# Differential and windowed attention: 128-row scores, rebuilt operand round trips, and PSUM shared as three and five banks

## The chip, the cores and the metric

The kernel runs on one core of one Trainium2 chip. The metric is device time in microseconds of one execution of the whole program, as the median of several runs. One execution was also recorded by the hardware profiler; all rows of the trace come from that one. The engines are TensorE (PE, with its weight loads as PEld), VectorE (DVE), ScalarE (ACT), GpSimd (POOL) and SyncE (SP), which here does no arithmetic and issues nearly all transfers.

## What is computed

Two layers of a bidirectional encoder trunk on 512 tokens of width 1024, all in float32. Each layer is, cut to what matters:

```
h = rms_norm(x)
z = h @ w_in                      # q, k, v of differential attention; q, k, v of three window groups; two gates
a = differential_attention(z_A)   # 4 heads, each with two 64-wide score maps: softmax(s0) - lambda * softmax(s1), times v
b = dilated_window_attention(z_B) # 3 groups x 8 heads of width 64, dilations 1, 4, 16; merged by softmax denominators
m = (sigmoid(g_A) * (a @ w_a) + sigmoid(g_B) * (b @ w_b)) @ w_out
x = x + rms_norm(m)
x = x + rms_norm(swiglu(rms_norm(x)))
```

Queries and keys get rotary embedding. A score is a product over 64 channels of a query and a key row. The kernel reaches float32 accuracy by splitting a number into a high part (`float32r`, rounded) and a low part (the remainder): a product of two split matrices is taken as hi x hi + hi x lo + lo x hi, three TensorE products (`mm3`, L120).

## The kernel before

The tokens are held in a permuted order, by their class modulo 4, so that the dilated groups see neighbours together; group 0 (dilation 1) needs the natural order. `class_rows` (L226) describes the permuted rows of a DRAM tensor; rows of x come in with `rows_in` (L229), four transfers of 32 rows per tile of 128 tokens, and leave at the end through `postnorm_tile` (L252), four per tile, one of them issued by GpSimd.

Weights stream from DRAM in 1 MB loads (`load_raw`, L85), are split by ScalarE and VectorE into high and low parts (`split_part`, L94), and are consumed in the order of `specs` (L321).

In a layer the first stage runs eight **units of projection**: for each half of the heads (u = 0, 1) one unit of differential attention (`da_proj`, L490), then for each half again three window groups (`g_proj`, L571). A unit projects q, k and v (`proj_qk`, `proj_v`), 48 TensorE products of 512 columns each for q and k and 96 of 256 columns for v. TensorE's order is written by hand: `drive` (L185) runs the projection as a generator and, at each of its yields (four for q, four for k, four for v), calls `att_step` (L169), which issues one step of an attention that was queued earlier. `att_push` gives each attention a delay in such steps (`DELAY`, L23: 4 for differential attention, 3 more for its first unit; 4, 2, 2 for groups 0, 1, 2). So the scores of a unit are issued a fixed number of steps after its last projection, between the products of the next units. The other engines and the transfers are ordered by a scheduler.

**The operand round trips.** A projection leaves the two rotary halves of four heads in partitions as (head, channel); the score products need channels on the partitions and the heads apart. Rope (L406) works on VectorE and GpSimd, and the result goes through DRAM scratch. In `qk_split` (L456), used by differential attention and by group 0, each of q and k is split into hi (L463, ScalarE) and lo (L465, VectorE), both are written to the scratch `dasc` (L466, L467), and loaded back in strips of 32 partitions (L474, L478, L481) into three operands: `QX` has, per head, hi and lo of q on 64 partitions each; `KX` has hi of k twice; `KL` has lo of k on 64 partitions. That makes 4 writes and 16 loads. `qk_scores` (L484) takes a score as two products: L487 contracts 128 rows (q hi and lo with k hi), L488 contracts 64 rows (q hi with k lo). A score call holds four such products, L487 and L488 in turn: two maps of 512 columns in differential attention, two windows of 256 columns in group 0. Each kind has 8 calls per unit, 2 units per layer and 2 layers.

Group 0 also sends v through the scratch `vd` (four writes, two loads, L575 to L581) into natural order, and its output back through `scr` and `scs` (`to_class`, L674). Its order is q, k, v. Groups 1 and 2 do without the split: `gsc` gets q and k in two writes, and four loads (L591) fetch both into `QK`; their scores (L616) contract 64 rows, sixteen products in a row.

All these transfers go through `move` (L423) to SyncE's queue. The operands live in the pool `big` (L429, 7 buffers of 8 KB per partition); `KL` and v live in `m4` (8 buffers).

**PSUM** has eight banks: four for projections (`pj`, L57) and four for attention (`at`, L60). `act_stationary` (L277), the last product of each sub-layer, uses all eight as accumulators, and `ws_halves` (L206) takes four projection banks for the first two products of the next stage.

Of the kernel before, what the change touches and what calls it, by code (L numbers as in the profile page):

```python
# [17 lines left out]
P = 128  # L18
D = 1024
S = 512  # L20
SPLIT_PRI = 400
MOVE_POOL = 0
DELAY = (4, 4, 2, 2, 3)  # L23
# [11 lines left out]
def encoder_trunk_kernel(  # L35
# [8 lines left out]
    depth = w_in.shape[0]  # L44
    mv = [0]

# [10 lines left out]
    def pj(shape=(P, S)):  # L57
        return ps.tile(list(shape), F32, tag="pj", name=nm("pj"))

    def at(shape=(P, S)):  # L60
        return ps.tile(list(shape), F32, tag="at", name=nm("at"))

# [143 lines left out]
    def ws_halves(jobs, tok_halves, between={}):  # L206
        step = S // tok_halves
        outs = [[pj() for _ in range(2)] for _ in jobs]
        made = {}
        for hf in range(tok_halves):  # L210
            sl = slice(hf * step, (hf + 1) * step)
            for jn, (o2, job) in enumerate(zip(outs, jobs)):
                lhs, rhs = made[jn] = made.get(jn) or job()
                for i in range(2):
                    mm3(o2[i][:, sl], [lhs(i, k) + (rh[:, sl], rl[:, sl]) for k, (rh, rl) in enumerate(rhs)])
                if (hf, jn) in between:
                    between[hf, jn]()
        return outs
# [10 lines left out]
    def rows_in(xt, src, n, permuted):  # L229
        if permuted:  # L230
            for s in range(4):
                nc.sync.dma_start(out=xt[32 * s:32 * s + 32, :], in_=class_rows(src, n)[s])
        else:
            nc.sync.dma_start(out=xt, in_=src[n * P:(n + 1) * P, :])

# [16 lines left out]
    def postnorm_tile(n, pe, src, g, dst, src_perm, dst_perm):  # L252
# [11 lines left out]
        nc.vector.scalar_tensor_tensor(out=xt, in0=t, scalar=r, in1=xt, op0=ALU.mult, op1=ALU.add)  # L264
        if dst_perm:
            for s in range(4):
                (nc.gpsimd if s == 3 else nc.sync).dma_start(out=class_rows(dst, n)[s], in_=xt[32 * s:32 * s + 32, :])
        else:
            nc.sync.dma_start(out=dst[n * P:(n + 1) * P, :], in_=xt)
        return xt, t  # L270
# [6 lines left out]
    def act_stationary(nk, lhs, post, turn, next_jobs):  # L277
        accs = [[(pj if n < 2 else at)() for _ in range(2)] for n in range(NT)]
        nch = nk // 2
# [41 lines left out]
    def specs():  # L321
# [11 lines left out]
        for l in range(depth):  # L333
            for u in range(2):
                yield from qkv(l, 256 * u, 512 + 256 * u, 1024 + 256 * u)[(1 if l == 0 and u == 0 else 0):]
            for u in range(2):
                for gi in range(3):
                    b = GB + gi * 1536 + 256 * u
                    yield from qkv(l, b, b + 512, b + 1024)

# [47 lines left out]
    for l in range(depth):  # L388
# [34 lines left out]
        def move(dst, src):  # L423
            mv[0] += 1
            eng = nc.gpsimd if MOVE_POOL and mv[0] % MOVE_POOL == 0 else nc.sync
            eng.dma_start(out=dst.bitcast(F32) if dst.dtype == F32R else dst,
                              in_=src.bitcast(F32) if src.dtype == F32R else src)

        def big(shape=(P, 4, S), dt=F32R):  # L429
            return ap.tile(list(shape), dt, tag="big", name=nm("big"), bufs=7)  # L430

# [23 lines left out]

        def qk_split(natural, first=None):  # L456
            QX, KX = big(), big()
            KL = m4([P, 2, S], F32R)
            sc = dp.tile([P, 2, 2, 2, S], F32, tag="dasc", name=nm("dasc"), bufs=2)
            for which in range(2):  # L460
                pair = rope((yield from proj_qk(which, first)), natural)
                hi = rt(F32R)
                nc.scalar.copy(out=hi, in_=pair)  # L463
                lo = rt(F32R)
                nc.vector.tensor_tensor(out=lo, in0=pair, in1=hi.bitcast(F32), op=ALU.subtract)  # L465
                move(sc[:, which, 0], hi)  # L466
                move(sc[:, which, 1], lo)  # L467
                src = sc.rearrange("(c j) w hl ab t -> w hl ab j c t", j=32)[which]
                if which == 0:
                    for hl in range(2):  # L470
                        for ab in range(2):
                            for par in range(2):
                                o = 64 * ((hl + par) % 2) + 32 * ab
                                move(QX[o:o + 32, par::2, :], src[hl, ab, :, par::2, :])  # L474
                else:
                    for ab in range(2):
                        for o in (32 * ab, 64 + 32 * ab):
                            move(KX[o:o + 32], src[0, ab])  # L478
                        for par in range(2):
                            o = 64 * par + 32 * ab  # L480
                            move(KL[o:o + 32], src[1, ab, :, par::2, :])  # L481
            return QX, KX, KL

        def qk_scores(o, qk, c, qs, ks):  # L484
            QX, KX, KL = qk
            b = 64 * (c % 2)
            nc.tensor.matmul(o, QX[:, c, qs], KX[:, c, ks], start=True, stop=False)  # L487
            nc.tensor.matmul(o, QX[b:b + 64, c, qs], KL[b:b + 64, c // 2, ks], start=False, stop=True)  # L488

        def da_proj(first):  # L490
            qk = yield from qk_split(False, first)
            return qk, (yield from proj_v())

# [77 lines left out]
        def g_proj(gi):  # L571
            if gi == 0:
                QK = yield from qk_split(True)
                v = yield from proj_v()
                vd = dp.tile([S, 256], F32, tag="vd", name=nm("vd"), bufs=2)  # L575
                for s in range(4):
                    move(vd.rearrange("(t s r) c -> s t r c", s=4, r=4)[s], v[32 * s:32 * s + 32])
                vn = m4([P, NT, 256])
                move(vn, vd.rearrange("(n p) c -> p n c", p=P))
                vs = m4([P, 3, 256])  # L580
                move(vs, vd[64:448].rearrange("(n p) c -> p n c", p=P))  # L581
                return QK, vn, vs
            QK = big((P, 2, 2, S), F32)
            sc = dp.tile([P, 2, 2, S], F32, tag="gsc", name=nm("gsc"), bufs=2)
            for which in range(2):
                move(sc[:, which], rope((yield from proj_qk(which, None)), False))
            src = sc.rearrange("(pair par j) w ab t -> par ab j w pair t", par=2, j=32)
            for par in range(2):
                for ab in range(2):
                    o = 64 * par + 32 * ab  # L590
                    move(QK[o:o + 32], src[par, ab])  # L591
            return QK, (yield from proj_v()), None

# [80 lines left out]
        def to_class(o, st):  # L674
# [4 lines left out]
            oc, sc = g_out(0)  # L679
            for s in range(4):  # L680
                move(oc[32 * s:32 * s + 32], scr.rearrange("(t s r) c -> s t r c", s=4, r=4)[s])
                move(sc[32 * s:32 * s + 32], scs.rearrange("(t s r) c -> s t r c", s=4, r=4)[s])
            return oc, sc
# [216 lines left out]
```

## Time and profile before

| what | value |
|---|---|
| median of 3 runs (lowest, highest) | 1938.34 us (1934.69, 1938.78) |
| the profiled execution | 1938.61 us |
| its span, first to last instruction | 1936.8 us |
| granted TensorE clock, mean of the span | 0.994 |
| DMA: all 16 engines, share of the span in which the hardware queue moved data | 41.2% |
| moved | 244.92 MB |

The median, not the mean, is the number to be predicted. In the page, "busy" is the time in which an engine worked on at least one instruction. TensorE's products overlap in the records: a product is shown until its result is out, while the next has begun, so its pace is read from start to start. In the view of waits, a row names the engine and the line that waited, what ended the wait, the total, the number of waits and the longest. In the rows of DMA issues the last number is the median time from issue to landing. In the table of windows the columns are the stretch, its length, the busy time of each engine with the number of its instructions, the granted clock, the busy share of the 16 DMA engines and GB/s.

### The profile page before, as it was taken

The numbers are of one execution on the slowest core, as the hardware profiler recorded it, in microseconds if no ns is written. First come the engines' busy times: TensorE is split into PE (matmuls) and PEld (weight loads), VectorE is DVE, ScalarE is ACT, GpSimd is POOL, SyncE is SP. The second block draws the span as 40 slices with busy tenths as digits, with TensorE's granted clock in tenths as the row PEclk, the third lists the DMA queues.
The fourth block names the chain that finished last, engine by engine and source line by source line (L and its number), as shares of the span: only waits on it lengthen the run. The fifth ranks groups of instructions, "written<-read, shape, count | busy, mean of one in ns | idle before, by whom it ended". The sixth has DMA issues, their size and how long they took to land. (4 is left out here: it accounts for less than half of the span.)

```text
span 1936.8 us, 24393 instructions
## 1 busy us (share of the span) xinstructions
PE 1889.4 (98%) x9952; PEld 1586.0 (82%) x9952; DVE 929.5 (48%) x1243; ACT 671.5 (35%) x1301; POOL 179.9 (9%) x136
## 2 busy tenths in 40 slices
PE   6999999999999999999999999999999999999997
PEld 6878887888888888888887788878888888888886
DVE  4676556544545333332366765556453453333222
ACT  3354333344224322221334544323432342222221
POOL 1111013011100000000011211121100000000000
PEclk9999999999999999999999999999999999999999
DMA  6844446442244332322448254554323432323232
GB/s 176 253 127 131 121 120 185 129 121 87 87 163 153 109 109 87 103 94 88 162 151 233 88 151 120 151 162 130 100 89 137 144 131 89 107 87 109 87 119 65
DMA packets 171871, 244.92 MB, mean 126 GB/s; under 512 B 10864, under 2 KB 136176, under 8 KB 171760
## 3 DMA queue, kind: packets, MB, share of 16 engines
q1 hardware_dynamic: 171568, 242.84, 41.2%
q8 instruction: 78, 1.28, 0.3%
q0 software_dynamic: 192, 0.52, 0.1%
q14 instruction: 33, 0.27, 0.0%
HBM read 205.52 MB, written 37.81 MB: 126 GB/s over the span
## 5 line engine op out<-in xcount | busy, mean ns | idle before, releaser
L123 PE MATMUL pj<-hTh,whi 128*128 128x512 f32 (+1 forms) x1600 | 610.1, 381 | 3.0 <-ACT hTh L248 3.0
L124 PE MATMUL pj<-hTl,whi 128*128 128x512 f32 (+1 forms) x1600 | 600.2, 375 | 6.0 <-DVE hTl L249 5.9
L125 PE MATMUL pj<-hTh,wlo 128*128 128x512 f32 (+1 forms) x1600 | 599.6, 375 | 0.0
L109 DVE TENSOR_TENSOR wlo<-raw,whi 128x1024 fp32r<-128x1024 f32 x252 | 341.1, 1355 | 489.4 <-ACT whi L108 480.4
L108 ACT CAST whi<-raw 128x1024 fp32r<-128x1024 f32 x252 | 264.7, 1051 | 771.2 <-PE pj L124 498.6
L123 PEld LDWEIGHTS pj<-hTh,whi 128*128 128x128 f32 x1600 | 304.0, 190 | 62.7 <-ACT hTh L248 5.2
L124 PEld LDWEIGHTS pj<-hTl,whi 128*128 128x128 f32 x1600 | 304.3, 190 | 58.0 <-DVE hTl L249 7.7
L125 PEld LDWEIGHTS pj<-hTh,wlo 128*128 128x128 f32 x1600 | 304.1, 190 | 54.6
L123 PE MATMUL pj<-whi,hTh 128*128 128x256 f32 x512 | 148.5, 290 | 0.0
L125 PE MATMUL pj<-whi,hTl 128*128 128x256 f32 x512 | 144.8, 283 | 0.0
L124 PE MATMUL pj<-wlo,hTh 128*128 128x256 f32 x512 | 144.8, 283 | 0.0
L634 ACT ACTIVATE e<-e,gst 128x128 f32<-128x128 f32 (+1 forms) x192 | 81.9, 428 | 140.0 <-DVE gst L631 139.9
L77 POOL TENSOR_TENSOR sm<-sm,mhalf 128x1 f32<-128x1 f32 (+1 forms) x48 | 28.7, 599 | 970.1 <-DVE sm L75 970.1
L123 PEld LDWEIGHTS pj<-whi,hTh 128*128 128x128 f32 x512 | 97.9, 191 | 6.0 <-issue 3.7
L124 PEld LDWEIGHTS pj<-wlo,hTh 128*128 128x128 f32 x512 | 98.0, 191 | 0.0
L125 PEld LDWEIGHTS pj<-whi,hTl 128*128 128x128 f32 x512 | 98.0, 191 | 0.0
L825 DVE TENSOR_TENSOR s<-s,pj 128x512 f32<-128x512 f32 x44 | 30.3, 689 | 123.7 <-PE pj L125 123.6
L420 POOL TENSOR_TENSOR r<-r,r 128x512 f32<-128x512 f32 x32 | 43.0, 1344 | 453.3 <-DVE r L418 332.8
L418 DVE TENSOR_TENSOR r<-pj,cos 128x512 f32<-128x512 f32 x48 | 32.9, 690 | 77.4 <-PE pj L125 77.4
L419 POOL TENSOR_TENSOR r<-r,r 128x512 f32<-128x512 f32 x32 | 64.5, 2015 | 25.0 <-DVE r L418 25.0
L487 PE MATMUL at<-big,big 128*128 128x256 f32 (+1 forms) x128 | 55.3, 432 | 9.6 <-DMA vd<-m 7.5
L287 PE MATMUL pj<-whi,ac 128*128 128x512 f32 x160 | 63.0, 394 | 0.0
(166 smaller groups left out, 2482.0 us busy)
## 6 DMA issues: line engine op xcount, KB each, us to landing
raw<-in_w_in_dram SPq DMA_DIRECT2D x64, 1024.0 KB, 7.0
raw<-in_w_gate_up_dram SPq DMA_DIRECT2D x44, 1024.0 KB, 5.1
raw<-in_w_down_dram SPq DMA_DIRECT2D x22, 1024.0 KB, 4.8
dasc<-r SPq DMA_DIRECT2D x32, 512.0 KB, 3.5
big<-dasc SPq DMA_DIRECT2D x64, 128.0 KB, 6.6
big<-dasc SPq DMA_DIRECT2D x32, 256.0 KB, 8.0
gsc<-r SPq DMA_DIRECT2D x16, 512.0 KB, 3.5
big<-gsc SPq DMA_DIRECT2D x32, 256.0 KB, 7.3
```

The source lines that it names most:

```text
L108: nc.scalar.copy(out=shp(hi), in_=src)
L109: nc.vector.tensor_tensor(out=shp(lo), in0=src, in1=shp(hi.bitcast(F32)), op=ALU.subtract)
L123: nc.tensor.matmul(o, ah, bh, start=(i == 0), stop=False)
L124: nc.tensor.matmul(o, ah, bl, start=False, stop=False)
L125: nc.tensor.matmul(o, al, bh, start=False, stop=(i == n - 1))
L287: nc.tensor.matmul(o, al, hi[:, sl], start=False, stop=False)
L418: nc.vector.tensor_tensor(out=dst[:, i], in0=u, in1=tb, op=ALU.mult)
L419: nc.gpsimd.tensor_tensor(out=pair[:, 0], in0=pair[:, 0], in1=tmp[:, 0], op=ALU.subtract)
L420: nc.gpsimd.tensor_tensor(out=pair[:, 1], in0=pair[:, 1], in1=tmp[:, 1], op=ALU.add)
L487: nc.tensor.matmul(o, QX[:, c, qs], KX[:, c, ks], start=True, stop=False)
L634: nc.scalar.activation(out=e[:, i, :], in_=e[:, i, :], func=AF.Exp, bias=sts[:, n, h:h + 1], accum_out=sts[:, n, 4 + h:5 + h])
L825: nc.vector.tensor_tensor(out=s, in0=s, in1=ou_[i], op=ALU.mult)
```

## The change

- `qk_split` becomes `split_part_of`, called once for q and once for k. The scratch holds hi and lo as 128 rows (part, rotary half, channel) by head. hi and lo are written by two transfers each, one per rotary half, and one transfer of 128 partitions fetches an operand. For k a second operand gets the same rows with the halves exchanged (two transfers of 64 partitions). Scores are then QX x KH + QX x KL with 128 rows in both products: hi x hi + lo x lo, and hi x lo + lo x hi. The product lo x lo is new.
- Group 0 projects k, v, q in this order (in `specs` and in `g_proj`).
- In groups 1 and 2, q and k are written by two transfers each (one per rotary half) and each is fetched by one.
- Rows of x, the last store, v in `vd` and the results in `scr` and `scs` take one transfer in the place of four; the last store leaves GpSimd's queue.
- PSUM: three `pj` banks and five `at` banks. `ws_halves` and `act_stationary` take their fourth projection bank from `at`.
- `big` has 8 buffers and holds K's low halves too; the scratch for DMA descriptors is set to 4096 bytes per partition.

```diff
@@ PSUM
-        return ps.tile(list(shape), F32, tag="pj", name=nm("pj"))
+        return ps.tile(list(shape), F32, tag="pj", name=nm("pj"), bufs=3)
...
-        return ps.tile(list(shape), F32, tag="at", name=nm("at"))
+        return ps.tile(list(shape), F32, tag="at", name=nm("at"), bufs=5)
...
-        outs = [[pj() for _ in range(2)] for _ in jobs]
+        outs = [[pj(), pj()], [pj(), at()]]
...
-        accs = [[(pj if n < 2 else at)() for _ in range(2)] for n in range(NT)]
+        accs = [[pj(), pj()], [pj(), at()], [at(), at()], [at(), at()]]
@@ rows of x, the last store
-        if permuted:
-            for s in range(4):
-                nc.sync.dma_start(out=xt[32 * s:32 * s + 32, :], in_=class_rows(src, n)[s])
-        else:
-            nc.sync.dma_start(out=xt, in_=src[n * P:(n + 1) * P, :])
+        nc.sync.dma_start(out=xt, in_=class_rows(src, n) if permuted else src[n * P:(n + 1) * P, :])
...
-                (nc.gpsimd if s == 3 else nc.sync).dma_start(out=class_rows(dst, n)[s], in_=xt[32 * s:32 * s + 32, :])
...
+        nc.sync.dma_start(out=class_rows(dst, n) if dst_perm else dst[n * P:(n + 1) * P, :], in_=xt)
@@ the order of the weights
-                    yield from qkv(l, b, b + 512, b + 1024)
+                    q, k, v = qkv(l, b, b + 512, b + 1024)
+                    yield from (k, v, q) if gi == 0 else (q, k, v)
@@ operands of differential attention and group 0 (qk_split goes)
+        def split_part_of(which, dsts, natural, first=None):
+            pair = rope((yield from proj_qk(which, first)), natural)
+            sc = dp.tile([P, 4, S], F32, tag="dasc", name=nm("dasc"), bufs=3)
+            rows = sc.rearrange("(hl ab j) c t -> hl ab c j t", hl=2, ab=2)
+            hi = rt(F32R)
+            nc.scalar.copy(out=hi, in_=pair)
+            for ab in range(2):
+                move(rows[0, ab], hi[:, ab, :])
+            lo = rt(F32R)
+            nc.vector.tensor_tensor(out=lo, in0=pair, in1=hi.bitcast(F32), op=ALU.subtract)
+            for ab in range(2):
+                move(rows[1, ab], lo[:, ab, :])
+            move(dsts[0], sc)
+            if len(dsts) > 1:
+                move(dsts[1][0:64], sc[64:128])
+                move(dsts[1][64:128], sc[0:64])
...
-            b = 64 * (c % 2)
-            nc.tensor.matmul(o, QX[:, c, qs], KX[:, c, ks], start=True, stop=False)
-            nc.tensor.matmul(o, QX[b:b + 64, c, qs], KL[b:b + 64, c // 2, ks], start=False, stop=True)
+            nc.tensor.matmul(o, QX[:, c, qs], KH[:, c, ks], start=True, stop=False)
+            nc.tensor.matmul(o, QX[:, c, qs], KL[:, c, ks], start=False, stop=True)
...
         def da_proj(first):
-            qk = yield from qk_split(False, first)
-            return qk, (yield from proj_v())
+            QX, KH, KL = big(), big(), big()
+            yield from split_part_of(0, (QX,), False, first)
+            yield from split_part_of(1, (KH, KL), False, first)
+            return (QX, KH, KL), (yield from proj_v())
@@ g_proj
-                QK = yield from qk_split(True)
+                QX, KH, KL = big(), big(), big()
+                yield from split_part_of(1, (KH, KL), True)
                 v = yield from proj_v()
                 vd = dp.tile([S, 256], F32, tag="vd", name=nm("vd"), bufs=2)
-                for s in range(4):
-                    move(vd.rearrange("(t s r) c -> s t r c", s=4, r=4)[s], v[32 * s:32 * s + 32])
+                move(vd.rearrange("(t s r) c -> s t (r c)", s=4, r=4), v.rearrange("p r c -> p (r c)"))
...
+                yield from split_part_of(0, (QX,), True)
+                return (QX, KH, KL), vn, vs
...
-                move(sc[:, which], rope((yield from proj_qk(which, None)), False))
-            src = sc.rearrange("(pair par j) w ab t -> par ab j w pair t", par=2, j=32)
-            for par in range(2):
-                for ab in range(2):
-                    o = 64 * par + 32 * ab
-                    move(QK[o:o + 32], src[par, ab])
+                pair = rope((yield from proj_qk(which, None)), False)
+                sc = dp.tile([P, 2, S], F32, tag="gsc", name=nm("gsc"), bufs=3)
+                for ab in range(2):
+                    move(sc.rearrange("(pj ab) pair t -> ab pair pj t", ab=2)[ab], pair[:, ab, :])
+                move(QK[:, which], sc)
@@ to_class
-            for s in range(4):
-                move(oc[32 * s:32 * s + 32], scr.rearrange("(t s r) c -> s t r c", s=4, r=4)[s])
-                move(sc[32 * s:32 * s + 32], scs.rearrange("(t s r) c -> s t r c", s=4, r=4)[s])
+            for dst, src in ((oc, scr), (sc, scs)):
+                move(dst.rearrange("p r c -> p (r c)"), src.rearrange("(t s r) c -> s t (r c)", s=4, r=4))
@@ kernel
-    nc = _bacc.Bacc("TRN2", target_bir_lowering=False, num_devices=1)
+    nc = _bacc.Bacc("TRN2", target_bir_lowering=False, num_devices=1, dynamic_dma_scratch_size=4096)
```

More of the change, by code (lines that the diff above doesn't have):

```diff
@@ L21 @@
 SPLIT_PRI = 400
-MOVE_POOL = 0
 DELAY = (4, 4, 2, 2, 3)
@@ L44, in encoder_trunk_kernel @@
     depth = w_in.shape[0]
-    mv = [0]
     pp = ctx.enter_context(tc.tile_pool(name="pp", bufs=1))
@@ L264, in postnorm_tile @@
         nc.vector.scalar_tensor_tensor(out=xt, in0=t, scalar=r, in1=xt, op0=ALU.mult, op1=ALU.add)
-        if dst_perm:
-            for s in range(4):
-                (nc.gpsimd if s == 3 else nc.sync).dma_start(out=class_rows(dst, n)[s], in_=xt[32 * s:32 * s + 32, :])
-        else:
-            nc.sync.dma_start(out=dst[n * P:(n + 1) * P, :], in_=xt)
+        nc.sync.dma_start(out=class_rows(dst, n) if dst_perm else dst[n * P:(n + 1) * P, :], in_=xt)
         return xt, t
@@ L423, in move @@
         def move(dst, src):
-            mv[0] += 1
-            eng = nc.gpsimd if MOVE_POOL and mv[0] % MOVE_POOL == 0 else nc.sync
-            eng.dma_start(out=dst.bitcast(F32) if dst.dtype == F32R else dst,
+            nc.sync.dma_start(out=dst.bitcast(F32) if dst.dtype == F32R else dst,
                               in_=src.bitcast(F32) if src.dtype == F32R else src)
         def big(shape=(P, 4, S), dt=F32R):
-            return ap.tile(list(shape), dt, tag="big", name=nm("big"), bufs=7)
+            return ap.tile(list(shape), dt, tag="big", name=nm("big"), bufs=8)
         oaT = [big() for i in range(2)]
@@ L454, in proj_v @@
             return v
[L456 to L470, printed above, removed]
-                        for ab in range(2):
-                            for par in range(2):
[L473 to L479, printed above, removed]
-                            o = 64 * par + 32 * ab
-                            move(KL[o:o + 32], src[1, ab, :, par::2, :])
-            return QX, KX, KL
@@ L484, in qk_scores @@
         def qk_scores(o, qk, c, qs, ks):
-            QX, KX, KL = qk
-            b = 64 * (c % 2)
-            nc.tensor.matmul(o, QX[:, c, qs], KX[:, c, ks], start=True, stop=False)
-            nc.tensor.matmul(o, QX[b:b + 64, c, qs], KL[b:b + 64, c // 2, ks], start=False, stop=True)
+            QX, KH, KL = qk
+            nc.tensor.matmul(o, QX[:, c, qs], KH[:, c, ks], start=True, stop=False)
+            nc.tensor.matmul(o, QX[:, c, qs], KL[:, c, ks], start=False, stop=True)
         def da_proj(first):
-            qk = yield from qk_split(False, first)
@@ L581, in g_proj @@
                 move(vs, vd[64:448].rearrange("(n p) c -> p n c", p=P))
-                return QK, vn, vs
+                yield from split_part_of(0, (QX,), True)
+                return (QX, KH, KL), vn, vs
             QK = big((P, 2, 2, S), F32)
-            sc = dp.tile([P, 2, 2, S], F32, tag="gsc", name=nm("gsc"), bufs=2)
             for which in range(2):
-                move(sc[:, which], rope((yield from proj_qk(which, None)), False))
-            src = sc.rearrange("(pair par j) w ab t -> par ab j w pair t", par=2, j=32)
-            for par in range(2):
+                pair = rope((yield from proj_qk(which, None)), False)
+                sc = dp.tile([P, 2, S], F32, tag="gsc", name=nm("gsc"), bufs=3)
                 for ab in range(2):
-                    o = 64 * par + 32 * ab
-                    move(QK[o:o + 32], src[par, ab])
+                    move(sc.rearrange("(pj ab) pair t -> ab pair pj t", ab=2)[ab], pair[:, ab, :])
+                move(QK[:, which], sc)
             return QK, (yield from proj_v()), None
@@ L679, in to_class @@
             oc, sc = g_out(0)
-            for s in range(4):
-                move(oc[32 * s:32 * s + 32], scr.rearrange("(t s r) c -> s t r c", s=4, r=4)[s])
-                move(sc[32 * s:32 * s + 32], scs.rearrange("(t s r) c -> s t r c", s=4, r=4)[s])
+            for dst, src in ((oc, scr), (sc, scs)):
+                move(dst.rearrange("p r c -> p (r c)"), src.rearrange("(t s r) c -> s t (r c)", s=4, r=4))
             return oc, sc
```

## The prediction

> **What bounds the kernel now.** First the totals of the page: the span, the busy shares, and TensorE's line in the forty slices.
>
> ```profile
> span 1936.8 us, 24393 instructions
> PE 1889.4 (98%) x9952; PEld 1586.0 (82%) x9952; DVE 929.5 (48%) x1243; ACT 671.5 (35%) x1301; POOL 179.9 (9%) x136
> PE   6999999999999999999999999999999999999997
> ```
>
> The profiled execution took 1938.61 us, 1.8 us more than its span and 0.3 us above the median of the three runs (1938.34), so I sum against 1938.6 and read the result as a median. TensorE is idle for 47.4 us of the span, mostly in the first and the last slice. Nothing that shortens another engine helps unless TensorE waits for it. Second, what TensorE's matmuls waited for (total us, times, longest):
>
> ```profile
> PE pj L246 <- DVE m L240: 13.9, 2, 10.8
> PE at L487 <- DMA vd<-m: 7.5, 2, 3.9
> PE pj L124 <- DVE hTl L249: 5.9, 7, 1.9
> PE at L616 <- DMA big<-gsc: 3.3, 3, 1.8
> PE pj L123 <- ACT hTh L248: 3.0, 7, 0.9
> PE at L487 <- ACT e L508: 1.7, 2, 0.8
> PE at L664 <- DVE e L642: 1.5, 2, 0.8
> ```
>
> The longest, 10.8 us, is the start of the program. Only 7.5 and 3.3 us belong to the round trips that the change rebuilds. A change here pays by making products shorter, or not at all. So, third, the timeline of TensorE around one score call of the differential attention (start, us, engine, line):
>
> ```profile
> 78.66 0.40 PE L487 MATMUL at<-big,big 128*128 128x512 f32 x1
> 78.99 0.49 PE L488 MATMUL at<-m,big 64*128 64x512 f32 x1
> 79.41 0.49 PE L487 MATMUL at<-big,big 128*128 128x512 f32 x1
> 79.83 0.50 PE L488 MATMUL at<-m,big 64*128 64x512 f32 x1
> 80.26 0.50 PE L123 MATMUL pj<-hTh,whi 128*128 128x512 f32 x1
> 80.60 0.39 PE L124 MATMUL pj<-hTl,whi 128*128 128x512 f32 x1
> 80.83 0.40 PE L125 MATMUL pj<-hTh,wlo 128*128 128x512 f32 x1
> ```
>
> The durations overlap, so read the starts. Two 128-row products of the projection start 0.23 us apart (80.60, 80.83). From L487 to the start of L124, five products take 1.94 us where five of those would take 1.15: 0.79 too much. Another call of that kind, which V's projection with 256 columns follows, and one of window group 0, where the scores have 256 columns too (the same six starts; those between are left out):
>
> ```profile
> 88.03 0.48 PE L487 MATMUL at<-big,big 128*128 128x512 f32 x1
> ...
> 89.95 0.28 PE L124 MATMUL pj<-wlo,hTh 128*128 128x256 f32 x1
> 90.07 0.28 PE L125 MATMUL pj<-whi,hTl 128*128 128x256 f32 x1
> ```
>
> ```profile
> 208.59 0.36 PE L487 MATMUL at<-big,big 128*128 128x256 f32 x1
> ...
> 210.04 0.28 PE L124 MATMUL pj<-wlo,hTh 128*128 128x256 f32 x1
> 210.16 0.28 PE L125 MATMUL pj<-whi,hTl 128*128 128x256 f32 x1
> ```
>
> The first takes 1.92 us where four at 0.23 and one at 0.12 (89.95, 90.07) would take 1.04: 0.88 too much. The second takes 1.45 (208.59 to 210.04) where five at 0.12 would take 0.60: 0.85. A 64-row product is not slow in itself, as a run of sixteen in groups 1 and 2 shows:
>
> ```profile
> 288.33 1.16 PE L616 MATMUL at<-big 64*128 64x128 f32 x16
> 289.42 0.50 PE L123 MATMUL pj<-hTh,whi 128*128 128x512 f32 x1
> ```
>
> Sixteen take 1.09 us. What costs is the **alternation** of 128 and 64 rows, some 0.2 us at each of the four changes of a call.
>
> **The change part by part.** *Scores.* All four products of a call get 128 rows, and as many columns as before. There are 32 calls of each kind (2 layers, 2 units, 8 calls each). If they run at the projections' pace, the gain is 32 x 0.79 to 0.88 plus 32 x 0.85, so 52.5 to 55.4, and I take **54 us** off the engine that sets the end. The bound below is nothing, if the cost is not the alternation (rival C); I take the full gain, because the 64 rows are all that sets these products apart in the rows. The 64-row products of L616 stay as they are.
>
> *Order k, v, q in group 0.* K and V, whose round trips are the longest, now have two projections behind them, and the 7.5 us go. But Q becomes late. These rows show Q's round trip in the second unit (products done at 288.33, above) and where the last projection of group 0 ends and its scores begin, in both units:
>
> ```profile
> 294.23 1.60 SPq L426 DMA_DIRECT2D dasc<-r  x2
> 299.33 3.63 SPq L426 DMA_DIRECT2D big<-dasc  x8
> 174.60 1.06 PE L532 MATMUL at<-m,e 128*128 128x128 f32 x8
> 189.54 0.36 PE L487 MATMUL at<-big,big 128*128 128x256 f32 x1
> 316.61 0.40 PE L123 MATMUL pj<-hTh,whi 128*128 128x512 f32 x1
> 327.53 0.60 PE L714 MATMUL at<-ident,m 128*128 128x128 f32 x4
> ```
>
> After the last product, rope and the cast take 5.9 us until the first write is issued, and the loads can go at +11.0. Now one load of 1 MB takes the place of eight; the nearest rows are loads of that size:
>
> ```profile
> raw<-in_w_in_dram SPq DMA_DIRECT2D x64, 1024.0 KB, 7.0
> raw<-in_w_out_dram SPq DMA_DIRECT2D x8, 1024.0 KB, 4.8
> gsc<-r SPq DMA_DIRECT2D x16, 512.0 KB, 3.5
> xs<-m SPq DMA_DIRECT2D x12, 512.0 KB, 2.9
> ```
>
> So Q lands 15.8 to 18.0 us after its last product. Scores begin 14.9 us after the last projection in the first unit (174.60 to 189.54) and some 11.3 in the second (316.61 to the end of the transposes at 327.9). TensorE waits 0.9 to 3.1 and 4.5 to 6.7 us, over two layers 11 to 19, for 7.5 before: **+3 to +12, I take +7**. All that TensorE has queued stands behind that wait, in the order written by hand. A weights load between write and load adds up to its own 4.8 us four times; I leave that to the upper end (+19).
>
> *Fewer, larger transfers.* A split operand pair needs 12 transfers where it needed 20, so SyncE issues less; it is not what TensorE waits for, so this is worth nothing by itself. The low halves of K are loaded whole, 0.5 MB more in each of 8 pairs, beside 245 MB. Groups 1 and 2 keep six transfers a pair, but Q's load no longer waits for K's write, and K's is one of 512 KB: the 3.3 us before L616 should go, **-3** (bounds 0 and -3.3). The first scores of a layer waited for no transfer; two larger loads in the place of eight small ones I put at 0, at worst the 4.8 us of one load per layer (+10). The rows of x, of vd and scr, and the last store become one transfer each; the first 10.8 us also need the gain row and VectorE, and I count 0. The last store loses GpSimd's share; 0. On SyncE the weights loads stand, as before, behind a write that waits for VectorE's low half, now one more write. [...]
>
> *PSUM.* Projections rotate over three banks in the place of four, so a bank must be empty two fills later, not three. Rope and the gates empty theirs early; V's copies are the exception:
>
> ```profile
> 59.59 0.40 PE L123 MATMUL pj<-hTh,whi 128*128 128x512 f32 x1
> 65.06 0.39 PE L123 MATMUL pj<-hTh,whi 128*128 128x512 f32 x1
> 76.95 1.05 ACT L453 COPY m<-pj 128x512 f32<-128x512 f32 x2
> ```
>
> V was done at 59.6, and ScalarE copied it at 76.95, because nobody needed the bank. With three banks the fill that starts at 65.06 needs it. ScalarE's order is not fixed by hand, and a copy that TensorE waits for must stand ahead of what needs later products, so I cost this at one or two of ScalarE's 1.05 us instructions: **+2** in all (0 to the rival below). Five attention banks remove no wait of the list: L508 and L642 are waits for data.
>
> Sum: -54 + 7 - 3 + 2 = -48, so 1938.6 - 48 = **1891 us**. Its own range takes all the low ends (-55.4 + 3 - 3.3 + 0, or 1883) and the high ones (-52.5 + 19 + 10 + 2, or 1917).
>
> **Rivals.** *A: the new writes are confined to few DMA engines* (slower). Every transfer of the kernel before starts, on both sides, with a count of 32 or 128. The new ones start on the DRAM side with 4 (hi and lo, x, vd, scr) or with 2 (groups 1 and 2). If the engines are dealt out by that count, 4 or 2 of 16 carry the write. In a stretch full of such traffic one engine moved 292 / (0.82 x 16) = 22.3 KB per us:
>
> ```profile
> 294.00:300.60 6.60, 5.86 (x31) 4.66 (x30) 6.29 (x11) 4.70 (x20) 0.00 (x0) 1.00 0.82 292
> ```
>
> Then an operand's hi and lo, 1049 KB over four, take 11.8 us where the loads could go 5.1 us after the first write: Q of group 0 lands 6.7 us later, four times (+27). Groups 1 and 2 write 524 KB over two, 11.8 us for 3.5: of the 8.3 us more, the single load gives back about 3, and group 2 has no slack before L616, so +5 four times, and the -3 is lost (+23). The first scores of each layer need K: up to 6.7 twice (+13). The first tile of x and the last store take 524 / 89 = 5.9 us for 2.9 (+6). Together +69, so **1960 us**. It decides from the point at which the added waits eat 48 us, two thirds of that price. For it speaks that the price needs only a count that the new access patterns have and the old ones had not; against it, that no transfer of the trace shows such a limit, as none has such a count.
> [...]
>
> *B: three banks bind.* V's copies stay where they stand on ScalarE, and TensorE waits for the bank from 65.06 to about 77.5, 12 us in each layer, and half as much where group 1's projection follows group 0's: +35, so **1926 us**. For it: the row at 76.95. Against: only the order of ScalarE keeps the copy back.
>
> *C: the alternation is not the cost*, for example because the second product re-reads the same bank. Then the sum is +6 without the 54: **1945 us**. Against it speaks that L123 to L125 also accumulate in one bank at 0.23 us.
>
> **How the numbers follow.** Forecast 0.47, A 0.33, B 0.09, C 0.05, and 0.06 for mixtures of the forecast with part of A, between 1917 and 1934. About 0.2% (4 us) can be told from no change. Faster: 0.47 + 0.09 + 0.06 and a tenth of A, less a little of B, 0.63; same 0.03; slower 0.34, most of A and all of C. The forecast's range alone holds 0.45; to reach eight in ten I take in B, the mixtures, C and the half of A up to 1963: 1882 to 1963.
>
> **What would show it.** In the profile after: L487 and L488 as 128-row products starting 0.23 and 0.12 us apart; TensorE busy near 1835 us; a wait of L487 for Q's load of some 5 us in the second unit and less in the first; no wait of L616. Writes of hi, lo and gsc landing in under 5 us from issue speak against A, over 8 us for it. Waits of L123 for ScalarE's L453 would be B. The prediction is wrong if the scores keep their pace, or if waits for transfers grow by more than 48 us.

## The result: 2011.95 us, 3.8% slower

| kernel | median | lowest to highest | runs |
|---|---|---|---|
| before | 1938.09 us | 1934.69 to 1938.78 | 4 |
| after | 2011.95 us | 2008.14 to 2014.19 | 4 |

After to before: 1.0383, 95% interval 1.0362 to 1.0403. The forecast was 1891, its range 1882 to 1963: the sign was wrong, and the time lies outside the range, above rival A's 1960.

First the totals of the page of the changed kernel, with TensorE's line in the forty slices and the granted clock:

```profile
span 2010.8 us, 24166 instructions
PE 1854.8 (92%) x9952; PEld 1590.7 (79%) x9952; DVE 926.9 (46%) x1243; ACT 670.1 (33%) x1301; POOL 178.0 (9%) x132
PE   3989799599999999999997979959999999999996
PEclk8989899799999999999998989989999999999998
```

TensorE is busy 34.6 us less than before (1889.4) and idle 156.0 us in the place of 47.4. The span grew by 74.0, which is 108.6 more idle less the 34.6. The two 5s and the 7s inside the span, where the kernel before has only 9s, say that this is a few long waits, and the clock falls in the same slices. The view of waits names them (total us, times, longest):

```profile
PE at L464 <- DMA big<-dasc: 78.5, 6, 20.8
PE pj L240 <- DVE m L234: 21.3, 2, 16.7
PE at L240 <- DVE m L234: 8.9, 1, 8.9
...
PE at L465 <- DMA big<-dasc: 6.3, 2, 3.2
PE at L594 <- DMA big<-gsc: 5.1, 2, 2.6
PE at L594 <- ACT whi L109: 2.7, 1, 2.7
PE at L594 <- ACT whi L106: 2.5, 1, 2.5
```

L464 and L465 are the two products of a score call (L487 and L488 before), L240 the transposes behind the first norm, L594 the scores of groups 1 and 2. No projection (L121) waits for a V copy. The groups by form split the waits of L464 (busy us, mean ns, then idle before them):

```profile
L464 PE MATMUL at<-big,big 128*128 128x512 f32 x64 | 29.0, 454 | 14.9 <-DMA big<-dasc 14.9
...
L464 PE MATMUL at<-big,big 128*128 128x256 f32 x64 | 20.5, 340 | 63.7 <-DMA big<-dasc 63.7
```

So of the 108.6 us: 63.7 before the 256-column scores of group 0 for 7.5, 21.2 before the 512-column ones (14.9 and L465's 6.3) for 1.7, 30.2 at the start for 13.9, 10.3 before L594 for 3.3. The last products of the two kernels, from their timelines, before first:

```profile
1926.44 0.40 PE L288 MATMUL at<-wlo,ac 128*128 128x512 f32 x1
```

```profile
1993.26 0.40 PE L278 MATMUL at<-wlo,ac 128*128 128x512 f32 x1
```

Behind them 10.0 us remained of the span before and 17.1 remain after: 7.1 more. The five differences sum to 106.1 of the 108.6.

One of the two longest waits, in the second unit of layer 0 (20.4 us; layer 1 has its like with 20.8), is the one to look at. TensorE's timeline, then the issues of SyncE:

```profile
374.04 0.55 PE L464 MATMUL at<-big,big 128*128 128x256 f32 x1 [20.38 <-DMA big<-dasc]
```

```profile
349.05 0.92 SPq L415 DMA_DIRECT2D m<-vd  x2
350.01 0.49 SPq L88 DMA_DIRECT2D raw<-in_w_in_dram  x1
350.60 6.73 SPq L415 DMA_DIRECT2D dasc<-r  x4
368.38 0.34 SPq L415 DMA_DIRECT2D big<-dasc  x1
```

The load of Q can go 17.8 us after its first write; before it was 5.1. Two loads of V and one of weights stand directly ahead of the four writes. (The landing times by which the prediction wanted to tell are not in this trace.) Now the table of windows of the same kernel: while these writes run, while TensorE resumes, and at the last store (the last three numbers: clock, busy share of the 16 DMA engines, GB/s):

```profile
358.00:367.00 9.00, 0.00 (x0) 0.00 (x0) 0.00 (x0) 0.00 (x0) 0.34 (x1) 0.53 0.26 101
374.00:379.00 5.00, 4.96 (x14) 4.12 (x15) 1.38 (x2) 1.09 (x4) 0.00 (x0) 0.50 0.45 138
379.00:385.00 6.00, 6.00 (x36) 5.12 (x35) 3.38 (x6) 2.74 (x6) 0.00 (x0) 1.00 0.36 131
1996.00:2008.00 12.00, 0.00 (x0) 0.00 (x0) 1.28 (x1) 0.00 (x0) 0.13 (x1) 0.54 0.25 92
```

0.26 of sixteen engines is as much as four at work, 25 GB/s each (101 over four). At the last store it is 0.25, and 23 each (92 over four). And the wait is not over when the data is there: for the next 5 us the granted clock is 0.50, and 14 products start where the following 6 us have 36.

### The profile page after: what moved, and what is told of

Read it like the earlier page. It is cut to its first block, busy times and chain, and to the rows that moved or that the text cites. A ratio compares the mean times of both kernels' runs of the same rounds, so it can differ in the third digit from the quotient of the medians.

```text
span 2010.8 us, 24166 instructions
## 1 busy us (share of the span) xinstructions
PE 1854.8 (92%) x9952; PEld 1590.7 (79%) x9952; DVE 926.9 (46%) x1243; ACT 670.1 (33%) x1301; POOL 178.0 (9%) x132
## 5 line engine op out<-in xcount | busy, mean ns | idle before, releaser
L121 PE MATMUL pj<-hTh,whi 128*128 128x512 f32 (+1 forms) x1536 | 593.6, 386 | 2.6 <-ACT hTh L242 2.6
L122 PE MATMUL pj<-hTl,whi 128*128 128x512 f32 (+1 forms) x1536 | 587.6, 383 | 7.6 <-DVE hTl L243 7.6
L123 PE MATMUL pj<-hTh,wlo 128*128 128x512 f32 (+1 forms) x1536 | 586.2, 382 | 0.0
L122 PEld LDWEIGHTS pj<-hTl,whi 128*128 128x128 f32 x1536 | 296.0, 193 | 61.2 <-DVE hTl L243 9.6
L121 PEld LDWEIGHTS pj<-hTh,whi 128*128 128x128 f32 x1536 | 296.6, 193 | 58.6 <-ACT hTh L242 5.1
L123 PEld LDWEIGHTS pj<-hTh,wlo 128*128 128x128 f32 x1536 | 295.7, 192 | 55.3
L121 PE MATMUL pj<-whi,hTh 128*128 128x256 f32 x512 | 145.8, 285 | 0.0
L464 PE MATMUL at<-big,big 128*128 128x256 f32 (+1 forms) x128 | 49.5, 397 | 78.5 <-DMA big<-dasc 78.5
L121 PEld LDWEIGHTS pj<-whi,hTh 128*128 128x128 f32 x512 | 97.9, 191 | 1.0
L464 PEld LDWEIGHTS at<-big,big 128*128 128x128 f32 x128 | 25.6, 200 | 82.2 <-issue 64.5
L411 POOL TENSOR_TENSOR r<-r,r 128x512 f32<-128x512 f32 x32 | 41.2, 1287 | 506.4 <-DVE r L409 366.9
L277 PE MATMUL at<-whi,ac 128*128 128x512 f32 x200 | 78.8, 394 | 0.0
L276 PE MATMUL at<-whi,ac 128*128 128x512 f32 x200 | 78.5, 392 | 0.0
```

Source lines behind the costliest of these rows:

```text
L121: nc.tensor.matmul(o, ah, bh, start=(i == 0), stop=False)
L122: nc.tensor.matmul(o, ah, bl, start=False, stop=False)
L123: nc.tensor.matmul(o, al, bh, start=False, stop=(i == n - 1))
L276: nc.tensor.matmul(o, ah, hi[:, sl], start=(k == 0), stop=False)
L277: nc.tensor.matmul(o, al, hi[:, sl], start=False, stop=False)
L411: nc.gpsimd.tensor_tensor(out=pair[:, 1], in0=pair[:, 1], in1=tmp[:, 1], op=ALU.add)
```

## The experiments

Theory A: transfers whose outermost count is 4 or 2 run on 4 or 2 engines, and what is late from that is the loss. The rivals: O, Q's place behind V costs, however fast the transfers are; B, the three banks; C, the score products did not get shorter.

Each ratio is to the kernel before, measured again beside the run (medians 1939.90 to 1940.47 us); a difference between two other kernels compares separate measurements, and some 2 us of it can come from that.

**The same kernel with every transfer spread.** hi and lo go out whole and come back in strips of 32 rows, and so do the group pairs; `vd`, `scr`, rows of x and the last store take four transfers of 32 rows again.

```diff
-            rows = sc.rearrange("(hl ab j) c t -> hl ab c j t", hl=2, ab=2)
...
-            for ab in range(2):
-                move(rows[0, ab], hi[:, ab, :])
+            move(sc[:, 0], hi)
...
-            move(dsts[0], sc)
+            src = sc.rearrange("(c j) hl ab t -> hl ab j c t", j=32)
+            for i, dst in enumerate(dsts):
+                for hl in range(2):
+                    for ab in range(2):
+                        o = 64 * (hl ^ i) + 32 * ab
+                        move(dst[o:o + 32], src[hl, ab])
```

> The changed kernel with every transfer's outermost count brought back to 32 or 128: hi and lo go out whole, one write of 128 rows each, and are loaded by 32-row strips (four for Q, eight for K); the pairs of groups 1 and 2, vd, scr, the rows of x and the last store likewise. The 128-row scores, the order k, v, q and the three and five banks stay. Theory A (the writes and the rows of x were confined to 4 or 2 of 16 DMA engines): the 64 us of waits before the 256-column scores fall to 11 to 19, the 21 us at the first scores of the layers and the 10 us before the group scores go, the start is back at some 16 us; 1883 to 1917, about 1891, which is the forecast's own sum. Theory O (what costs is Q's place behind V, however fast a transfer is): 40 us or more of the wait before the 256-column scores stay, and the time is 1940 or above. Theory B (three banks): waits of TensorE's projections for V's copies, 1926.

Measured: 1919.05 us (1917.85 to 1922.88), ratio to before 0.9889 (0.9870 to 0.9909). That is 92.9 us less than the changed kernel, and theory O falls with it. It is 28 us more than the forecast, though, and 2 us above what theory A allowed here. The groups by form (L471 and L472 are the scores here):

```profile
L471 PE MATMUL at<-big,big 128*128 128x512 f32 x64 | 28.4, 443 | 6.7 <-ACT e L494 3.9 <-DMA big<-dasc 1.9 <-ACT e L509 0.4
L472 PE MATMUL at<-big,big 128*128 128x512 f32 x64 | 26.0, 406 | 4.6 <-DMA big<-dasc 4.6
L471 PE MATMUL at<-big,big 128*128 128x256 f32 x64 | 20.5, 340 | 26.5 <-DMA big<-dasc 21.6 <-issue 4.9
```

26.5 us still stand before group 0's scores ("issue" is idle time for which the trace shows no releaser). SyncE's issues at the first of them:

```profile
173.04 0.34 SPq L423 DMA_DIRECT2D dasc<-r  x1
173.47 0.92 SPq L88 DMA_DIRECT2D raw<-in_w_in_dram  x1
175.64 0.34 SPq L423 DMA_DIRECT2D dasc<-r  x1
176.12 7.11 SPq L423 DMA_DIRECT2D big<-dasc  x4
```

A weights load (L88) stands between the two writes of Q, and the four loads take 7.1 us to issue, since two of them need the second write. It is the case that the prediction left to its upper end. It holds for the first units, with 9.9 of the 26.5 us. In the second units, with 16.6, no weights load stands there, but V's two loads do:

```profile
313.90 1.60 SPq L423 DMA_DIRECT2D dasc<-r  x2
315.72 1.22 SPq L423 DMA_DIRECT2D m<-vd  x2
317.00 2.46 SPq L423 DMA_DIRECT2D big<-dasc  x4
```

How much of the wait is theirs was not tried.

**The scores' edit alone**, in the kernel before (the diff leaves out the loads, 12 strips of 32 rows for 16, the size of `big`, the descriptor space and the last store, all of it on SyncE):

```diff
-            KL = m4([P, 2, S], F32R)
+            KL = big()
...
-            b = 64 * (c % 2)
...
-            nc.tensor.matmul(o, QX[b:b + 64, c, qs], KL[b:b + 64, c // 2, ks], start=False, stop=True)
+            nc.tensor.matmul(o, QX[:, c, qs], KL[:, c, ks], start=False, stop=True)
```

> The kernel before with nothing but the scores' edit: Q once as hi over lo, K twice as hi over lo and lo over hi, all four products of a call at 128 rows; the order q, k, v, four and four banks, writes of 128 rows and loads of 32-row strips stay as they were (the last store is issued by SyncE alone, and K's second operand is a big buffer). The forecast's first term: 52.5 to 55.4 us less, 1883 to 1886. Theory C (the alternation of 128 and 64 rows is not the cost): within 4 us of the kernel before.

Measured: 1947.86 us (1941.78 to 1955.28), ratio 1.0030 (1.0012 to 1.0047): no gain at all, and neither answer as it was put. C does not hold, since the products did get shorter: in the trace of this kernel the calls quoted in the prediction with 1.92 and 1.45 us have medians of 1.13 and 0.67. The gain went into three things that were smaller or not there before. TensorE is idle 82.0 us for 47.4. It is busy 53.9 us at clock 0.50 for 15.9; half of the difference, 19 us, is what that costs by estimate. And the 512-column calls before projections of 512 columns fell only to 1.71 us, with waits for ScalarE's copies out of attention banks (L514) in most of them (ten waits, 4.0 us), of which there are four here. The largest waits for transfers (L478, L479 scores, L653 values of group 0):

```profile
PE at L479 <- DMA big<-dasc: 9.5, 3, 4.5
PE at L653 <- DMA m<-vd: 8.6, 2, 4.3
PE at L478 <- DMA big<-dasc: 6.9, 3, 4.0
```

The long products had been covering round trips, and copies out of the banks.

**The changed kernel in the order q, k, v**, its writes left confined (two lines in `specs` and `g_proj`).

> The changed kernel with group 0 back in the order q, k, v, its writes left as they are. Theory A: the writes still take 11 to 12 us; K's round trip now has only V's projection (about 11 us) behind it, so the wait of 64 us before the 256-column scores falls by some 11 us at each of four places, and V's own write and loads become late for the values; with all other waits left, 1960 to 1985. Theory O: nearly all of the 64 us goes, and the time is 1950 or less.

Measured: 1970.93 us (1969.54 to 1971.71), 41 us less than after, as theory A had it; the 256-column scores wait 22.0 us for 63.7.

**Counts by themselves.** Behind the kernel before, which is left as it was, one buffer is written and read back with its rows dealt out differently; these transfers are no part of what is computed.

```diff
+    for k, rows in ((1, 128), (32, 128), (16, 128), (8, 128), (4, 128), (2, 128), (3, 96), (6, 96), (24, 120), (17, 119)):
+        part = spare[0:rows].rearrange("(b a) c -> a b c", a=k)
+        nc.sync.dma_start(out=part, in_=buf[0:rows])
+        nc.sync.dma_start(out=buf, in_=spare)
```

> The kernel before, and behind its last store eleven writes of one buffer of 128 rows of 4 KB to a scratch in DRAM, each followed by a plain load of it. Only the order in which the rows are dealt out differs, so that the outermost count on the DRAM side is 128, 32, 16, 8, 4 and 2 (512 KB each), 3 and 6 (96 rows, 384 KB), 24 (120 rows) and 17 (119 rows); the last load has the count of 4 on its DRAM side. Theory A: while a write runs, the busy share of the 16 engines is near 1 for 128, 32 and 16, 0.5 for 8, 0.25 for 4, 0.13 for 2, 0.19 for 3, 0.38 for 6, and the writes take in proportion: with the 100 GB/s of four engines in the changed kernel's trace 5 us for the count of 4, 10 us for 2, 2.6 for 8, each with some 2 us of fixed time; the load with a count of 4 is as slow as the write. If the engines are dealt out by a common divisor of both sides, 24 takes 12 engines (0.75) and 17 a single one (0.06, 19 us). Rival: the slowness lies in the size or the order of the pieces, and all writes of 512 KB take the same time within 1 us.

The windows inside the writes with 8, 4, 2 and 17, and inside the load with 4, in this order (the last two numbers: share, GB/s):

```profile
1953.00:1956.00 3.00, 0.00 (x0) 0.00 (x0) 0.00 (x0) 0.00 (x0) 0.00 (x0) 0.50 0.47 124
1963.00:1969.00 6.00, 0.00 (x0) 0.00 (x0) 0.00 (x0) 0.00 (x0) 0.00 (x0) 0.50 0.23 66
1976.00:1985.00 9.00, 0.00 (x0) 0.00 (x0) 0.00 (x0) 0.00 (x0) 0.00 (x0) 0.50 0.13 46
...
2023.00:2041.00 18.00, 0.00 (x0) 0.00 (x0) 0.00 (x0) 0.00 (x0) 0.00 (x0) 0.50 0.06 25
2048.00:2052.00 4.00, 0.00 (x0) 0.00 (x0) 0.00 (x0) 0.00 (x0) 0.00 (x0) 0.50 0.26 100
```

The shares follow the count: 0.47, 0.23 and 0.13 for 8, 4 and 2. The windows of the others give 0.90 and 0.87 for 32 and 16, 0.17 for 3 and 0.34 for 6. With 17, on a side of 119 rows, it is 0.06 of sixteen, as much as one engine at work, at 25 GB/s. The write takes 21.5 us (issue to the next issue):

```profile
2020.97 0.66 SPq L858 DMA_DIRECT2D spare<-m  x1
2042.48 0.33 SPq L859 DMA_DIRECT2D m<-spare  x1
2046.13 0.58 SPq L861 DMA_DIRECT2D m<-spare  x1
2053.80 0.32 SPq L862 DMA_DIRECT2D spare<-m  x1
```

The last pair is the load with a count of 4 on its DRAM side, 7.7 us. The load before it, plain and of the same size, took 3.7 (2042.48 to 2046.13). The share inside it is 0.26, so this read was confined as the writes were. For the count of 24 the window from 2014.4 to 2016.4 us, in its write, gives 0.61, which does not settle whether 12 engines carried it. That a common divisor of both sides decides is not shown here: only the DRAM side's count was chosen. The rival, by which all writes of 512 KB take the same time, falls: they took from 3.1 us (count 32) to 12.8 us (count 2). The times themselves I had wrong: the write with 4 took 10.1 us where I expected 5 and some 2 of fixed time, at 66 GB/s where the changed kernel's four engines move 101. Its rows lie apart in DRAM; whether that is the reason was not tried.

**One group of transfers spread at a time**, the rest as changed: hi and lo (the diff of the first experiment), the rows of x with last store, `vd` and `scr`, and the writes of groups 1 and 2:

```diff
-                    move(sc.rearrange("(pj ab) pair t -> ab pair pj t", ab=2)[ab], pair[:, ab, :])
+                    for k in range(2):
+                        move(sc.rearrange("(pj ab) pair t -> ab pair pj t", ab=2)[ab, k],
+                             pair[64 * k:64 * k + 64, ab, :])
```

> The changed kernel with hi and lo alone brought back to whole writes of 128 rows and loads of 32-row strips; the confined writes of groups 1 and 2, of vd and scr, the rows of x and the last store stay as changed. Theory A, by the rows of the changed kernel's waits: to the 1919 us of the kernel with every transfer spread come back the 16 us at the start (its first two and its third tile), some 8 us behind the last product and the 10 us before the group scores, with a half clock for a few us behind each, so 1950 to 1965. If hi and lo were not the main cost: above 1985.

> The changed kernel with the rows of x, the last store, vd and scr alone brought back to four transfers of 32 rows; hi, lo and the group pairs stay confined. Theory A: the 16 us at the start and some 8 us behind the last product go, with up to 5 us of the half clock behind the start's waits, all of the rest stays: 1982 to 1990. Rival: the start waits for the weights and the gain row and the end for the norm, and both stay: 2005 or above.

> The changed kernel with the writes of groups 1 and 2 alone cut so that their outermost count is 64 in the place of 2 (four writes of 128 KB for an operand in the place of two of 256 KB). Theory A: the 10 us of waits before the group scores go with the 14 us of half clock behind them, and Q's load of the second unit's group 0 stands behind less traffic: 1985 to 2003. If these waits are not the writes' (two of the four are put down to casts of weights): 2007 or above.

| spread alone | median (lowest to highest) | less than after |
|---|---|---|
| hi and lo | 1973.44 (1970.34 to 1974.62) | 38.5 |
| rows of x, last store, `vd`, `scr` | 1971.08 (1969.49 to 1974.58) | 40.9 |
| writes of groups 1 and 2 | 1997.83 (1996.63 to 2000.75) | 14.1 |
| all | 1919.05 | 92.9 |

The three sum to 93.5: the three groups are the whole of this difference, and their parts add up. The third came as expected, the first 8 us above and the second 11 us below. The rows are worth more than the start and the end: group 0's waits, 63.7, fall with them too, to 52.1; the start's waits of 30.2 are 11.5 there. The row of group 0:

```profile
L472 PE MATMUL at<-big,big 128*128 128x256 f32 x64 | 20.5, 340 | 52.1 <-DMA big<-dasc 29.2 <-issue 23.0
```

In the third kernel the scores of groups 1 and 2 do not wait: its list of waits has no row for them.

**Four and four banks**, transfers spread, order k, v, q.

> The kernel with every transfer spread and the order k, v, q, with PSUM back at four projection and four attention banks. The forecast's term for three banks was +2, theory B's +35; no projection of the changed kernel waits for V's copies, so here the time should stay within 4 us of the 1919 us with three and five banks. Theory B: 1890 or less. If the fifth attention bank had a use that no list of waits shows: 1925 or more.

Measured: 1934.96 us (1932.47 to 1936.15), 15.9 us more than with three and five. B falls for good, and the fifth attention bank has a use. Two rows of its groups by form, against 6.7 and 26.5 above:

```profile
L471 PE MATMUL at<-big,big 128*128 128x512 f32 x64 | 29.8, 465 | 10.5 <-ACT e L509 4.4 <-ACT e L494 3.8 <-DMA big<-dasc 1.6
L471 PE MATMUL at<-big,big 128*128 128x256 f32 x64 | 20.5, 340 | 33.0 <-DMA big<-dasc 24.6 <-issue 8.4
```

The 4.4 us are twelve waits for L509, the copy out of an attention bank, where five banks had two with 0.4: that is the missing bank. Shorter waits of this kind are in no list. The trace shows them in the length of the calls: before projections of 512 columns the median of all 16 calls is 1.72 us here and 1.24 with five banks, which makes 7.7 us. Why Q's loads also come later (33.0) is open.

**The order q, k, v**, transfers spread, three and five banks.

> The kernel with every transfer spread and three and five banks, group 0 in the order q, k, v. The forecast's term for the order k, v, q was +7 (its own range +3 to +19), so by it this kernel takes 1900 to 1916. Against it stand the waits of the kernel with the scores' edit alone, which has this order: K's second strips and V's rows were late there in 30 us of waits; by these the order k, v, q is the better one once the scores are short, and this kernel takes 1925 to 1940.

Measured: 1935.47 us (1932.57 to 1939.63), 16.4 us more than with k, v, q. The forecast's sign for the order is wrong once the scores are short. The values of group 0 (L650) wait for V here:

```profile
PE at L650 <- DMA m<-vd: 13.2, 4, 5.9
```

**Later scores.** Two numbers in the list of delays. They are counted in the steps of the hand-written order; a step is half of the products that fill one projection bank, and the texts below call it a half projection:

```diff
-DELAY = (4, 4, 2, 2, 3)
+DELAY = (4, 7, 2, 2, 4)
```

> The kernel with every transfer spread, three and five banks and the order k, v, q, and the scores of group 0 put three half projections later in TensorE's order (those of the first differential unit one later). If the 26 us of waits before the 256-column scores and the 5 us before the first 512-column ones are latency of the round trips that no product covers, they go, with the half clock behind them (27 us at half, so some 10): 1880 to 1893. Rival: the loads are held back by what stands ahead of them on SyncE, whose order moves along with the scores, and the waits return: above 1908.

Measured: 1901.29 us (1900.26 to 1902.41). The waits before group 0's scores are gone (one wait of 1.6 us for an operand is left, at a 512-column score), but 15.1 us of projections waiting for casts of weights on ScalarE took part of their place, so the time lies between the two answers. The last number put back to 3:

> As the last kernel (transfers spread, three and five banks, k, v, q, the scores of group 0 three half projections later), but the first differential unit's scores where they were. The 7 us twice in which a projection waited for ScalarE's casts of the weights, with exponentials of the second unit standing ahead of them, came with that one step; they go, with the half clock behind them (17 us at half), and the 5 us at the first scores of the two layers come back: 1882 to 1895. Rival: the casts wait because group 0's steps push what follows: 1898 or above.

Measured: 1884.20 us (1880.54 to 1888.06), ratio to before 0.9715 (0.9692 to 0.9738): the best of all, faster than both kernels. The busy line of its page, and the one row of waits of scores for transfers above 1 us:

```profile
PE 1833.4 (98%) x9952; PEld 1573.9 (84%) x9952; DVE 926.8 (49%) x1243; ACT 668.5 (36%) x1301; POOL 179.7 (10%) x132
```

```profile
PE at L472 <- DMA big<-dasc: 4.4, 2, 2.5
```

**The changed kernel with later scores**, its transfers left confined (`DELAY` is 4, 12, 2, 2, 7).

> The changed kernel, its confined transfers left as they are, with the scores of group 0 eight half projections later and those of the first differential unit four later. If the confined writes cost only latency, later scores cover it: of the 85 us of waits at the scores nearly all goes, with the half clock behind them, and the time is 1905 to 1935 (the start, the group pairs and the last store stay slow). If they also hold SyncE's queue and so the weights, waits of projections take their place: above 1960.

Measured: 1964.87 us (1964.24 to 1966.42). That is the second answer's time, above 1960, and not its mechanism: no projection waits for weights. The waits of scores for transfers fell from 85 us to 0.9, as the first answer has it, so they were latency that other products can cover. But TensorE now waits for the softmax stages behind the scores:

```profile
PE at L624 <- ACT e L612: 19.7, 2, 9.9
PE at L500 <- DVE e L494: 14.1, 2, 7.3
```

## Why the prediction was wrong

**The step that failed** is the sentence on fewer, larger transfers, "worth nothing by itself", with the 0 beside it for the rows of x, `vd`, `scr` and the last store. The forecast priced the new transfers by loads of their size, 2.9 to 7.0 us, and those rows all had 128 or 32 as outermost count. They cost 93 us: confined to 4 and 2 of 16 engines (0.26 in the window above; 0.23 and 0.13 for counts of 4 and 2 by themselves), they were late where TensorE needed them. The right mechanism was in the text, as rival A, and it got 0.33; its argument against, that no transfer of the trace showed such a limit since none had such a count, was no argument at all.

**Rival A was mis-sized too**: 1960 for 2012, its price +69 on the forecast where 121 came. One engine was taken at 22.3 GB/s and moved 25 (101 over four), so the rate was about right. Wrong was what hangs on it. From the first write of Q to its load A had 11.8 us, and it took 17.8 in the wait above: A left out what stands ahead of the writes. Group 0's Q was +27 and its waits grew from 7.5 to 63.7, which is 49 above the forecast's own 14.5 (7.5 and the 7); the rows of x and the last store were +6 and are 16.3 and 7.1, because three tiles of x came late and not one (waits of 16.7, 4.6 and 8.9 us for 10.8 and 3.1); the first scores were +13 and are 19.5; groups 1 and 2 were +23 and are 10.3 in waits, 14.1 with what follows. No half clock was in it: TensorE is busy 51.9 us at clock 0.50 for 15.9 before.

**The scores: right, a little too large.** The timeline of the changed kernel:

```profile
187.63 0.47 PE L464 MATMUL at<-big,big 128*128 128x512 f32 x1
...
188.64 0.39 PE L121 MATMUL pj<-hTh,whi 128*128 128x512 f32 x1
188.87 0.39 PE L122 MATMUL pj<-hTl,whi 128*128 128x512 f32 x1
```

Five products take 1.24 us (187.63 to 188.87) for 1.94 in the call quoted before. Over the calls without a wait the medians fell from 2.05 to 1.24 and from 1.92 to 1.13 (512 columns, before a projection of 512 or of 256 columns) and from 1.57 to 0.79 and 1.45 to 0.67 (256 columns), with 16 calls of each: 16 x 3.16 = 50.6 us for the 54 forecast. The alternation was the cost. (A little of the 2.05 is not: some of these calls also had short waits for a copy out of an attention bank.)

**The rest of the sum, read from the kernel with every transfer spread** (span 1921.1 us, TensorE busy 1849.3): Q last +19 (26.5 for 7.5), the upper end, in the first units for the weights load between write and load that I had seen and put aside, in the second units with V's loads there, which I had not seen; the 512-column scores +10 (11.3 for 1.7), of it 6.5 for transfers, where I took 0 and allowed 10, and 3.9 for exponentials (L494) that free an attention bank, where I had nothing; the group scores -3 as forecast; three banks no wait, and with five attention banks a gain of 15.9 that I had denied. TensorE's busy time fell by 40.1 and not by 50.6. The 10.5 us between them are by estimate slower clock, a term that the sum did not have: TensorE is busy 40.1 us at clock 0.50 there and 15.9 before, and half of that difference is 12.1. -50.6 + 24.4 of idle time + 10.5 = -15.7, the difference of the spans. The upper end itself was summed wrongly: four times 4.8 us are 19 by themselves, and added to Q's +12 they give +31, so the range of the sum should have ended at 1929 and not at 1917; the stated range went beyond both. With all waits but a few covered, TensorE is busy 1833.4 us; the prediction's sign for that was "near 1835".

**Order.** I priced k, v, q against waits of the kernel before, as if they stayed. They belong to long scores. With short ones the old order has its own waits, for V and K, and loses by 16.4; with the confined writes it won by 41.

## What to carry to other kernels

Count the outermost dimension before merging transfers: here DMAs with 4 on their DRAM side kept 0.23 to 0.26 of sixteen engines busy, as much as some four, and one with 17, against 119 rows, 0.06, as much as one. Where an engine at 98% is made faster, list the round trips and bank copies that its work covers, and move the consumers later in the same edit: the scores' edit alone brought nothing; with spread transfers and group 0's scores three half projections later it is part of a kernel that is 2.9% faster. Price a wait of some us with the half clock that can follow it: here 3.3 us at 0.50 behind a wait of 2.55 us.

## What the runs showed of the hardware

The clock after a wait. In the changed kernel half the clock followed a wait of 2.55 us (timeline, then the window behind it):

```profile
305.93 1.16 PE L594 MATMUL at<-big 64*128 64x128 f32 x16 [2.55 <-DMA big<-gsc]
```

```profile
307.40:310.70 3.30, 3.30 (x9) 2.61 (x8) 2.18 (x5) 1.69 (x9) 0.00 (x0) 0.50 0.15 50
```

Nine products start in these 3.3 us. Shorter waits went both ways in this kernel: of two of 1.88 us, ended at 649.7 and at 1019.4 us, the first left the clock at 1.00, and 3.4 us at 0.50 came after the second. Over the whole kernel the same matmuls were busy 1854.8 us after and 1833.4 us in the best kernel, 21.4 us apart; at clock 0.50 they were busy 51.9 and 3.0 us, and half of that difference is 24.4.
